# A two-layer hybrid decoder trunk on one NeuronCore: x^T kept by halves of K, one set of sum operands moved, two more weight load buffers

## The chip, the cores and the metric

The kernel runs on one core of one Trainium2 chip. TensorE (PE in the profile, its weight loads PEld), VectorE (DVE), ScalarE (ACT), GpSimd (POOL) and SyncE (SP) run their own instruction streams in order and meet through semaphores; 16 DMA engines move data between HBM and SBUF. SP issues one queue of DMAs and POOL another. The metric is device time in microseconds for the whole program. The kernel before takes 2170.99 us (median of 3 runs, 2167.93 to 2171.49). The profile is of one further execution, which took 2173.16 us.

## The reference

Two post-norm layers on 256 tokens of width 2048, all in float32:

```python
for i in range(DEPTH):                                  # DEPTH = 2
    mix = _hybrid_mixer(x, positions, w_in[i], g_cq[i], g_ckv[i], w_uq[i], w_ukv[i], w_o[i])
    x = _layer_norm(ALPHA * x + mix, ln1_g[i], ln1_b[i])
    ffn = _swiglu(x, w_gate[i], w_up[i], w_down[i])      # FFN_DIM = 5632
    x = _layer_norm(ALPHA * x + ffn, ln2_g[i], ln2_b[i])

def _swiglu(x, w_gate, w_up, w_down):
    h = silu(einsum('bsd,df->bsf', x, w_gate)) * einsum('bsd,df->bsf', x, w_up)
    return einsum('bsf,fd->bsd', h, w_down)
```

The mixer is one input projection, sparse attention over 64 selected keys, latent attention, and an output projection; the change does not touch its arithmetic. It bears on the feed-forward part (`_swiglu`).

## The kernel before

Precision comes from splitting: each float32 operand is a high part in float32r and a low part, and a product of two operands is three matmuls (high by high, high by low, low by high). ScalarE writes the high part of a weight tile (`wh`, line 336), VectorE subtracts it to get the low part (`wl`, line 337). A weight unit is 128 partitions x 1024 values, which is two K tiles of 128 by 512 columns, 512 KB.

**Buffers.** `load_raw` fetches a unit on SP's queue into a `raw` buffer. In the feed-forward part there are 8 of these: `RAW` = 4 that are there throughout and `RAWMORE` = 4 in a pool that is opened for this part (phase "more"). `some` deals them out by a fixed pattern. Seven `wh`/`wl` pairs (`UNITS` 5 and `MORE` 2) hold split units. `load_sum` fetches two units into a `sum` buffer on POOL's queue, the second added in flight; there are two such buffers. Eight-kilobyte tiles (`t8`) form a ring of 10: the two token tiles of x, x^T as `xh` and `xl` for both token tiles, one `few`, and the hidden activations `hT`.

**Feed-forward part.** FFN columns are cut into 11 chunks of 512 (`fc` 0 to 10). A chunk of gate and up is computed in four "quads", each taking one pair of K units, u and u + 4. A *plain* quad loads four units and uses each for both token tiles. A *sum* quad (`wino_quad`, "S") uses Winograd's form of Strassen: seven products instead of eight, each of one unit against one 128-token operand, p1, p2, p3, p6, p7, p4, p5 in this order. It loads three units (r11, r21, r22) and one sum (r12), and VectorE makes the other weights in place: r11 becomes r12 + r11 (line 1038), r21 becomes r11 + r21 (line 1045), r22 becomes r11 - r22 (line 1050). So the buffer of r11 is released only when line 1050 has read it. Some of the stationary operands are sums of quarters of x^T too; `sum_operands` makes them (`many` for K tiles 4 to 7, `few` for 2 and 3, a second `few` for 0 and 1). A *made* quad ("Q") reads weight sums that were made in the attention part and stored in HBM (`q`). Chunks 4 to 10 have the order S S Q S and use no plain quad; chunk 3 has S S plain S.

The products of a sum quad take as stationary operand token tile 0 with the low half of K (p1), token tile 0 with the high half (p2), token tile 1 with the high half (p4), and sums (the others). Token tile 1 with the low half of K is in no product of a sum quad.

From chunk 3 on, half of a `down` product (`down_half`, two columns of 512, 16 units, results added to x by POOL's DMAs `x<-d`) precedes each chunk's gate and up. `first_operands`, which makes the second `few`, is called between the two columns of the half before chunk 3.

**Order.** A list scheduler orders each engine's stream from the program's order, priorities and its own cost figures; `tc.high_priority` puts the closing VectorE additions of a chunk (`e`, `g`, line 1020) ahead. Streams are in order, so an instruction that waits holds back all behind it on its engine.

Of the kernel before, what the change touches and what calls it, by code (L numbers as in the profile page):

```python
# [25 lines left out]
F32R = mybir.dt.float32r  # L26
I32 = mybir.dt.int32
AF = mybir.ActivationFunctionType
ALU = mybir.AluOpType
# [3 lines left out]
P = 128  # L33
D = 2048
S = 256
NT = S // P
DEPTH = 2
# [15 lines left out]
KU = 2  # L53
C = 512
NKT = D // P
NFC = FFN // C
RAW = 4
UNITS, MORE = 5, 2
RAWMORE, RAWSUM = 4, 2
HALF = NKT // KU // 2  # L60
SOONER = 60
SOON = 200
# [2 lines left out]
ALLFROM, EARLY = 4, 0  # L65
# [17 lines left out]
def hybrid_trunk(ctx: ExitStack, tc: tile.TileContext, x, xt_in, pos, w_in, g_cq, g_ckv, w_uq,  # L83
                 w_ukv, w_o, ln1_g, ln1_b, ln1_T, w_gu, w_down, ln2_g, ln2_b, ln2_T, out):
    nc = tc.nc
# [7 lines left out]
    def nm(s):  # L93
        uid[0] += 1
        return f"{s}{uid[0]}"

    def t8(shape, dt, s):
        return sb.tile(shape, dt, name=nm(s), tag="a8", bufs=10)


    phase = {"name": None, "pool": None, "cm": None, "n": 0}
# [17 lines left out]
    def t2(shape, s, dt=F32):  # L119
        if phase["name"] == "att":  # L120
            phase["t2"] = phase.get("t2", 0) + 1
            if phase["t2"] * T2MORE % (T2 + T2MORE) < T2MORE:
                return pt(shape, dt, s, "t2", T2MORE)
        return sb.tile(shape, dt, name=nm(s), tag="t2", bufs=T2)
# [17 lines left out]
    def trp():  # L142
        return in_turn("tr", 4, 2)

    def att():

        return ps.tile([P, 2, C], F32, name=nm("att"), tag="b67", bufs=1)
# [3 lines left out]
    def f(ap):  # L151
        return ap.bitcast(F32)


    xt = [t8([P, D], F32, "x") for _ in range(NT)]
    xh = [t8([P, NKT, P], F32R, "xh") for _ in range(NT)]
    xl = [t8([P, NKT, P], F32R, "xl") for _ in range(NT)]

    def load_xT(u):

        ks = slice(KU * u, KU * u + KU)
        s = t2([P, NT, KU, P], "xs")
        nc.sync.dma_start(s, xt_in[u])
        for t in range(NT):
            split(xh[t][:, ks, :], xl[t][:, ks, :], s[:, t])

    def load_x():
        for t in range(NT):
# [100 lines left out]
    def step(task):  # L269
        try:  # L270
            task[0] = units_gone[0] + (next(task[1]) or 1)
        except StopIteration:
            tasks.remove(task)
# [7 lines left out]
    def spawn(gen):  # L281
        task = [0, gen]
        tasks.append(task)
        step(task)
        return task
# [90 lines left out]
    def transpose4(srcs, psum):  # L376
        for i, s in enumerate(srcs):
            nc.tensor.transpose(psum[:, i * P:(i + 1) * P], s, ident)  # L378

    def split(hi, lo, src):  # L380
        nc.scalar.activation(hi, src, AF.Copy)
        nc.vector.tensor_tensor(lo, src, f(hi), op=ALU.subtract)

    def xlhs(xh, xl):
        return lambda t, k: (xh[t][:, k, :], xl[t][:, k, :])

    def moments(y):

        st = small([P, D // C, 6], "bnst")
        for c in range(D // C):  # L390
            nc.vector.bn_stats(st[:, c, :], y[:, c * C:(c + 1) * C])
        mv = small([P, 2], "bnmv")
        nc.vector.bn_aggr(mv, st.rearrange("p c s -> p (c s)"))
        rs = small([P, 1], "bnrs")
        ve = small([P, 1], "bnve")
        nc.vector.tensor_scalar(ve, mv[:, 1:2], LN_EPS, None, ALU.add)
        nc.gpsimd.tensor_tensor(rs, ve, mhalf, op=ALU.pow)
        return mv[:, 0:1], rs

    def normalise(y, m):  # L400

        mu, rs = m
        for c in range(D // C):
            sl = slice(c * C, (c + 1) * C)
            nc.vector.tensor_scalar(y[:, sl], y[:, sl], mu, rs, ALU.subtract, ALU.mult)
            yield c, sl

    def norm_T(gbT, y, hi, lo, wait):


        for _ in normalise(y, moments(y)):
            pass
        yield wait
        pair = att()
        for c in range(D // C):
            tp = trp() if c < 2 else pair[:, c - 2, :]
            transpose4([y[:, c * C + i * P:c * C + (i + 1) * P] for i in range(4)], tp)
            v = t2([P, 4, P], "v")
            for i in range(4):
                k = 4 * c + i  # L420
                nc.scalar.activation(v[:, i, :], tp[:, i * P:(i + 1) * P], AF.Identity,
                                     bias=gbT[:, 1, k:k + 1], scale=gbT[:, 0, k:k + 1])
            nc.vector.tensor_copy(hi[:, 4 * c:4 * c + 4, :], v)
            nc.vector.tensor_tensor(lo[:, 4 * c:4 * c + 4, :], v, f(hi[:, 4 * c:4 * c + 4, :]), op=ALU.subtract)  # L424
            yield 1

    def load_gbT(src):
        gbT = sb.tile([P, 2, NKT], F32, name=nm("gbT"), tag="gbT", bufs=2)
        nc.gpsimd.dma_start(gbT, src)
        return gbT  # L430
# [97 lines left out]
        split(oh.rearrange("p j t -> p (j t)"), ol.rearrange("p j t -> p (j t)"), op)  # L528


    def layer(l, xh, xl, norms, last):
        xk = xlhs(xh, xl)

        def in_chunk(b, before=None, split_t=None):
            n = IN_BLOCKS[b][1]
# [303 lines left out]
        m = mla_half(0)  # L839
# [5 lines left out]
        m = mla_half(1)  # L845
# [20 lines left out]
        def many(shape):  # L866

            return phase["pool"].tile(shape, F32R, name=nm("many"), tag="many", bufs=1)
# [24 lines left out]
        finish(early)  # L893
        turn("more")
        gbT = load_gbT(ln1_T[l])
        xh, xl, norms = [], [], []

        def then(t):
            xh.append(t8([P, NKT, P], F32R, "xh"))
            xl.append(t8([P, NKT, P], F32R, "xl"))  # L900
            norms.append(spawn(norm_T(gbT, xt[t], xh[t], xl[t], 5 if t else 6)))

        last_pass(lambda c, k: w_o[l, c, k // KU], [4, 6], olhs, then)


        xk = xlhs(xh, xl)

        def gu(i, fc, split_t=None):
            return proj([(w_gu[i][l, fc, u], range(u * KU, (u + 1) * KU)) for u in range(NKT // KU)], xk, C,
# [1 line left out]

        sums = {}

        def sum_operands(*groups):


            for k0, n, where in groups:
                def x(t, i):
                    ks = slice(k0 + i * NKT // 2, k0 + i * NKT // 2 + n)
                    v = t2([P, n, P], "av")  # L920
                    nc.vector.tensor_tensor(v, f(xh[t][:, ks, :]), f(xl[t][:, ks, :]), op=ALU.add)
                    return v

                def diff(i, y, z):
                    v = t2([P, n, P], "sv")
                    nc.vector.tensor_tensor(v, y, z, op=ALU.subtract)
                    hi, lo = where[:, i, 0], where[:, i, 1]
                    split(hi, lo, v)
                    for k in range(n):
                        sums[f"s{i + 1}", k0 + k] = hi[:, k, :], lo[:, k, :]  # L930
                    return v

                a21 = x(1, 0)
                s1 = diff(0, a21, x(1, 1))
                a11 = x(0, 0)
                s2 = diff(1, a11, s1)
                diff(2, a21, a11)
                diff(3, x(0, 1), s2)
# [143 lines left out]
        def down(pair, cols, between=None):  # L1082


            fcs, hTs = [h[0] for h in pair], [h[1] for h in pair]
            finish(*[h[2] for h in pair])
            per = C // P // KU
            for i, c in enumerate(cols):
                o = proj([(w_down[l, c, per * fcs[0] + u], range(u * KU, (u + 1) * KU))
                          for u in range(per * len(fcs))], down_lhs(hTs), C, None, None, (0, 1) if i % 2 else (2, 3))  # L1090
                for t in range(NT):
                    d = t2([P, C], "d")
                    nc.scalar.activation(d, o[t], AF.Copy)  # L1093
                    nc.gpsimd.dma_start(xt[t][:, c * C:(c + 1) * C], d, accum_op=ALU.add)  # L1094
                if i == 0 and between:
                    between()
# [8 lines left out]
        held = []  # L1105
# [4 lines left out]
            held.append((fc, hT, spawn(hidden(g, u, hT, wait))))  # L1110

        def first_operands():
            sum_operands((0, 2, phase["pool"].tile([P, 4, 2, 2, P], F32R, name=nm("few"), tag="few", bufs=1)))

        def down_half(fc):

            down(held[:2], (0, 1) if fc % 2 else (2, 3), first_operands if fc == ALLFROM - 1 else None)
            if fc % 2 == 0:
                del held[:2]

# [6 lines left out]
        g = gu(0, 0, lambda: finish(*norms))  # L1127
        affine(ln1_g[l], ln1_b[l], 0, ALPHA)
        u = gu(1, 0)
        sum_operands((4, 4, many([P, 4, 2, 4, P])), (2, 2, t8([P, 4, 2, 2, P], F32R, "few")))  # L1130
        affine(ln1_g[l], ln1_b[l], 1, ALPHA)
        spawn_hidden(0, g, u)
        for fc in range(1, NFC):
            order = ORDER.get(fc, "SSQS")
            if fc >= FIRSTD:
                down_half(fc)
                finish_hidden()
            g, u = gate_up(fc, [({"N": "plain", "S": "wino", "Q": "made"}[k], v) for k, v in zip(order, UNIT[order])],
                           finish_hidden if fc < FIRSTD else None)
            if fc < FIRSTD:  # L1140
                affine(ln1_g[l], ln1_b[l], fc + 1, ALPHA)
            spawn_hidden(fc, g, u)
        xh, xl, norms, ms = [], [], [], []
        if last:
            gb = gains()
        else:
            gbT = load_gbT(ln2_T[l])
# [5 lines left out]
        if last:  # L1153
            for t in range(NT):
                norm_out(t, gb, ms[t])
        return xh, xl, norms

    norms = []
    for l in range(DEPTH):
        xh, xl, norms = layer(l, xh, xl, norms, l == DEPTH - 1)  # L1160
    turn(None)


# [48 lines left out]
```

## Time and profile before

| | |
|---|---|
| median of 3 runs | 2170.99 us |
| profiled execution | 2173.16 us |
| its span, first to last instruction | 2171.4 us |
| PE busy | 2139.9 us, 99% |
| DVE busy | 1848.9 us, 85% |
| ACT busy | 1288.8 us, 59% |
| POOL busy | 300.4 us, 14% |
| DMA queues, share of 16 engines | SP's 52.4%, POOL's 25.9% |
| mean granted TensorE clock | 0.997 |

A busy PE is not PE at its peak: matmuls overlap and their ends are modelled (a 512-column matmul is listed with 389 ns, but the next starts 227 ns later). So a stage's length says more than its busy share. Stages are cut here at the first matmul of a gate and up chunk (`gu_` tiles) and of a down half (`acc<-wh,hT`); chunks 4 to 10 of the first layer lie between 602 and 1012 us, those of the second between 1680 and 2092 us.

### The profile page before, as it was taken

The page shows a single profiled execution, that of the slowest core. Times are in us where ns is not written, and L with a number is a line of the kernel's source. Part 1 is how long each engine was busy: PE and PEld are TensorE (multiplying, and loading weights), DVE is VectorE, ACT ScalarE, POOL GpSimd, SP SyncE. Part 2 cuts the span into 40 slices and gives each one's busy share as a digit, 9 for nine tenths or more (in the row PEclk, how much of TensorE's full clock was granted, in tenths as well). Part 3 has the DMA queues.
Part 4 walks back from the last instruction along what each step waited for, and adds up shares of the span by engine and source line. Part 5 has one row for each costly group of instructions (what it writes and reads, how often), then busy time and mean ns, then how long its engine had stood idle before and what let it go on. Part 6 is the DMA issues. An engine that isn't in the chain of part 4 may idle for free.

```text
span 2171.4 us, 28387 instructions
## 1 busy us (share of the span) xinstructions
PE 2139.9 (99%) x9948; PEld 1768.8 (81%) x9948; DVE 1848.9 (85%) x2361; ACT 1288.8 (59%) x1675; POOL 300.4 (14%) x494
## 2 busy tenths in 40 slices
PE   8999999999999999999999999999999999999997
PEld 7888888888888878878888888888888888878876
DVE  6696776999989999999767976779998999989985
ACT  5555544666666667666455555446666666666663
POOL 0122220011011111110102122200011011111101
PEclk9999999999999999999999999999999999999999
DMA  8687888567888988887656877875678898888884
GB/s 299 206 295 273 294 292 280 175 203 244 260 258 265 281 266 267 269 281 255 203 180 227 292 275 280 315 247 174 210 250 256 272 270 261 275 266 268 286 311 106
DMA packets 158832, 552.97 MB, mean 255 GB/s; under 512 B 17904, under 2 KB 18208, under 8 KB 158048
## 3 DMA queue, kind: packets, MB, share of 16 engines
q1 hardware_dynamic: 111744, 401.79, 52.4%
q0 software_dynamic: 46800, 149.23, 25.9%
q8 instruction: 78, 1.28, 0.2%
q14 instruction: 66, 0.54, 0.1%
q10 hardware_dynamic: 144, 0.13, 0.0%
HBM read 498.12 MB, written 31.46 MB: 244 GB/s over the span
## 4 chain that ended last, share of the span: by engine, by line
PE 78%; DVE 11%; issue 5%; DMA 4%; ACT 1%; POOL 0%; SPq 0%; DVEq 0%; POOLq 0%; ACTq 0%
PE acc L359 16%; PE acc L358 16%; PE acc L360 16%; DVE wl L337 5%; PE gu_p L983 3%; PE gu_p L984 3%; PE gu_p L981 3%; DMA raw<-in_w_up_dram 3%; PE tr L378 2%; PE gu_c L981 2%; PE gu_c L984 2%; PE gu_c L983 2%; PE att L981 1%; PE att L984 1%; PE att L983 1%
## 5 line engine op out<-in xcount | busy, mean ns | idle before, releaser
L336 ACT ACTIVATE wh<-raw 128x1024 fp32r<-128x1024 f32 (+1 forms) x910 | 937.5, 1054 | 637.7 <-PE acc L360 220.9
L337 DVE TENSOR_TENSOR wl<-raw,wh 128x1024 fp32r<-128x1024 f32 (+1 forms) x910 | 1078.7, 1214 | 222.9 <-ACT wh L336 218.1
L358 PE MATMUL acc<-wh,xh 128*128 128x512 f32 (+1 forms) x768 | 302.9, 395 | 5.9 <-ACT wh L336 5.9
L359 PE MATMUL acc<-wl,xh 128*128 128x512 f32 (+1 forms) x768 | 297.5, 388 | 0.8 <-DVE wl L337 0.8
L360 PE MATMUL acc<-wh,xl 128*128 128x512 f32 (+1 forms) x768 | 297.4, 388 | 0.0
L359 PE MATMUL acc<-wl,hT 128*128 128x512 f32 x640 | 251.2, 392 | 0.5
L358 PE MATMUL acc<-wh,hT 128*128 128x512 f32 x640 | 250.0, 391 | 0.0
L360 PE MATMUL acc<-wh,hT 128*128 128x512 f32 x640 | 249.8, 390 | 0.0
L358 PEld LDWEIGHTS acc<-wh,xh 128*128 128x128 f32 x768 | 144.6, 188 | 37.0 <-ACT wh L336 7.1
L359 PEld LDWEIGHTS acc<-wl,xh 128*128 128x128 f32 x768 | 144.8, 189 | 28.9 <-DVE wl L337 2.9
L360 PEld LDWEIGHTS acc<-wh,xl 128*128 128x128 f32 x768 | 144.6, 188 | 28.3 <-DVE xl L424 0.6
L359 PEld LDWEIGHTS acc<-wl,hT 128*128 128x128 f32 x640 | 120.5, 188 | 30.4 <-DVE wl L337 5.8
L358 PEld LDWEIGHTS acc<-wh,hT 128*128 128x128 f32 x640 | 120.4, 188 | 25.3
L360 PEld LDWEIGHTS acc<-wh,hT 128*128 128x128 f32 x640 | 120.5, 188 | 24.7
L983 PE MATMUL gu_c<-wl,xh 128*128 128x512 f32 x360 | 140.3, 390 | 0.3 <-DVE wl L337 0.3
L981 PE MATMUL gu_c<-wh,xh 128*128 128x512 f32 x360 | 140.1, 389 | 0.0
L984 PE MATMUL gu_c<-wh,xl 128*128 128x512 f32 x360 | 140.1, 389 | 0.0
L1094 POOL DMA_DIRECT2D x<-d x80 | 69.5, 907 | 349.9 <-ACT d L1093 347.8
L315 POOL DMA_DIRECT2D sum<-in_w_up_dram x56 | 30.9, 552 | 533.6 <-DVE wl L337 501.6
L983 PE MATMUL gu_p<-wl,many 128*128 128x512 f32 x240 | 95.0, 396 | 8.6 <-DVE wl L337 8.4
L984 PE MATMUL gu_p<-wh,many 128*128 128x512 f32 x240 | 93.5, 390 | 0.0
L981 PE MATMUL gu_p<-wh,many 128*128 128x512 f32 x240 | 93.4, 389 | 0.0
(297 smaller groups left out, 3773.8 us busy)
## 6 DMA issues: line engine op xcount, KB each, us to landing
raw<-in_w_gate_dram SPq DMA_DIRECT2D x176, 512.0 KB, 5.9
raw<-in_w_down_dram SPq DMA_DIRECT2D x176, 512.0 KB, 7.7
raw<-in_w_in_dram SPq DMA_DIRECT2D x144, 512.0 KB, 5.2
sum<-in_w_up_dram POOLq DMA_DIRECT2D x112, 512.0 KB, 7.4
raw<-in_w_up_dram SPq DMA_DIRECT2D x106, 512.0 KB, 5.5
raw<-in_w_o_dram SPq DMA_DIRECT2D x64, 512.0 KB, 5.8
q<-q POOLq DMA_DIRECT2D x56, 512.0 KB, 4.1
raw<-q SPq DMA_DIRECT2D x56, 512.0 KB, 6.5
```

What stands on the lines that cost most here:

```text
L315: nc.gpsimd.dma_start(raw, a)
L336: nc.scalar.activation(wh[:, :n], raw[:, :n], AF.Copy)
L337: nc.vector.tensor_tensor(wl[:, :n], raw[:, :n], f(wh[:, :n]), op=ALU.subtract)
L358: mm(o[t][:, :n], h, a, start=first, stop=False)
L359: mm(o[t][:, :n], h, b, start=False, stop=False)
L360: mm(o[t][:, :n], l, a, start=False, stop=final)
L378: nc.tensor.transpose(psum[:, i * P:(i + 1) * P], s, ident)
L981: mm(o[name], h, a, start=name not in begun, stop=False)
L983: mm(o[name], h, b, start=False, stop=False)
L984: mm(o[name], l, a, start=False, stop=end)
L1094: nc.gpsimd.dma_start(xt[t][:, c * C:(c + 1) * C], d, accum_op=ALU.add)
```

## The change

x^T of a token tile is no longer one tile of high parts and one of low parts, each over all 16 K tiles, but one tile for the lower half of K and one for the upper, each with high and low parts (`halves`, `x_parts`). `first_operands` moves one chunk later, to the down half before chunk 4, and its tile (`few`, 8 KB) is no longer in the pool of the feed-forward part but a tile of the ring of 10, allocated after the first sum has read token tile 1 with the lower half of K. `RAWMORE` goes from 4 to 6: 10 raw buffers instead of 8, with the same 8 KB of the pool.

```diff
-RAWMORE, RAWSUM = 4, 2
+RAWMORE, RAWSUM = 6, 2
...
-    xh = [t8([P, NKT, P], F32R, "xh") for _ in range(NT)]
-    xl = [t8([P, NKT, P], F32R, "xl") for _ in range(NT)]
+
+    def halves():
+
+        return [t8([P, 2, NKT // 2, P], F32R, "xhl") for _ in range(2)]
+
+    xT = [halves() for _ in range(NT)]
+
+    def x_parts(x, k, n):
+
+        ks = slice(k % (NKT // 2), k % (NKT // 2) + n)
+        return tuple(x[k // (NKT // 2)][:, i, ks, :] for i in range(2))
...
-    def xlhs(xh, xl):
-        return lambda t, k: (xh[t][:, k, :], xl[t][:, k, :])
+    def xlhs(xT):
+        return lambda t, k: tuple(m[:, 0, :] for m in x_parts(xT[t], k, 1))
...
+        def few():
+            return t8([P, 4, 2, 2, P], F32R, "few")
+
         def sum_operands(*groups):
 
 
-            for k0, n, where in groups:
+            for k0, n, place in groups:
                 def x(t, i):
-                    ks = slice(k0 + i * NKT // 2, k0 + i * NKT // 2 + n)
                     v = t2([P, n, P], "av")
-                    nc.vector.tensor_tensor(v, f(xh[t][:, ks, :]), f(xl[t][:, ks, :]), op=ALU.add)
+                    hi, lo = x_parts(xT[t], k0 + i * NKT // 2, n)
+                    nc.vector.tensor_tensor(v, f(hi), f(lo), op=ALU.add)
                     return v
...
                 a21 = x(1, 0)
+                where = place()
                 s1 = diff(0, a21, x(1, 1))
...
         def first_operands():
-            sum_operands((0, 2, phase["pool"].tile([P, 4, 2, 2, P], F32R, name=nm("few"), tag="few", bufs=1)))
+
+            sum_operands((0, 2, few))
 
         def down_half(fc):
 
-            down(held[:2], (0, 1) if fc % 2 else (2, 3), first_operands if fc == ALLFROM - 1 else None)
+            down(held[:2], (0, 1) if fc % 2 else (2, 3), first_operands if fc == ALLFROM else None)
...
-        sum_operands((4, 4, many([P, 4, 2, 4, P])), (2, 2, t8([P, 4, 2, 2, P], F32R, "few")))
+        sum_operands((4, 4, lambda: many([P, 4, 2, 4, P])), (2, 2, few))
```

PE's instructions keep their order throughout. On VectorE, the place to look at is the first layer's sum quad that is split ahead while a down half runs. Before, in the half before chunk 3 (`raw_5130`, `raw_5132`, `raw_5134` are that quad's r11, r21, r22; `av` and `sv` are the sums of x^T, `few` their low parts):

```order
L1038 TENSOR_TENSOR raw_5130<-sum_5127,raw_5130 128x1024
L921 TENSOR_TENSOR av_5009<-xh_3781,xl_3782 128x256
L921 TENSOR_TENSOR av_5011<-xh_3781,xl_3782 128x256
L337 TENSOR_TENSOR wl_5159<-raw_5134,wh_5158 128x1024
L926 TENSOR_TENSOR sv_5013<-av_5009,av_5011 128x256
L1045 TENSOR_TENSOR raw_5132<-raw_5130,raw_5132 128x1024
L382 TENSOR_TENSOR few_5008<-sv_5013,few_5008 128x256
```

Now, in the half before chunk 4 (`raw_5642`, `raw_5644`, `raw_5646` are r11, r21, r22 of chunk 4's first quad):

```order
L1049 TENSOR_TENSOR raw_5642<-sum_5639,raw_5642 128x1024
L931 TENSOR_TENSOR av_5520<-xhl_3781 128x256
L931 TENSOR_TENSOR av_5523<-xhl_3782 128x256
L345 TENSOR_TENSOR wl_5671<-raw_5646,wh_5670 128x1024
L936 TENSOR_TENSOR sv_5525<-av_5520,av_5523 128x256
L1056 TENSOR_TENSOR raw_5644<-raw_5642,raw_5644 128x1024
L390 TENSOR_TENSOR few_5522<-sv_5525,few_5522 128x256
```

The twelve operations on x^T moved as a block by one chunk; the weight operations between them stand as they did.

On SP, the end of chunk 4's loads in the first layer. Before (`raw_5810` to `raw_5814` and the `q` loads are the made quad, `raw_5897`, `raw_5899`, `raw_5901` the last sum quad's r11, r21, r22):

```order
L309 DMA raw_5850<-q_1317 128x1024
L309 DMA raw_5852<-q_1315 128x1024
L309 DMA raw_5899<-in_w_gate_dram 128x1024
L309 DMA raw_5897<-in_w_gate_dram 128x1024
L309 DMA raw_5901<-in_w_up_dram 128x1024
L309 DMA raw_5991<-in_w_down_dram 128x1024
L309 DMA raw_6009<-in_w_down_dram 128x1024
```

Now:

```order
L317 DMA raw_5850<-q_1317 128x1024
L317 DMA raw_5852<-q_1315 128x1024
L317 DMA raw_5897<-in_w_gate_dram 128x1024
L317 DMA raw_5899<-in_w_gate_dram 128x1024
L317 DMA raw_5991<-in_w_down_dram 128x1024
L317 DMA raw_5901<-in_w_up_dram 128x1024
L317 DMA raw_6009<-in_w_down_dram 128x1024
```

r11 stands first again, and the quad's third load has one `down` load moved ahead of it. Elsewhere on this queue single neighbours trade places in the same way.

On VectorE, the end of the first layer's attention part, where the last units of `w_o` are split (`own` tiles hold two of them). Before:

```order
L337 TENSOR_TENSOR own_3594<-raw_3601,own_3594 128x1024
L337 TENSOR_TENSOR wl_3420<-raw_3417,wh_3419 128x1024
L337 TENSOR_TENSOR own_3605<-raw_3612,own_3605 128x1024
L337 TENSOR_TENSOR wl_3438<-raw_3435,wh_3437 128x1024
L337 TENSOR_TENSOR wl_3460<-raw_3457,wh_3459 128x1024
```

Now, some ten rows later in VectorE's stream:

```order
L345 TENSOR_TENSOR wl_3577<-raw_3574,wh_3576 128x1024
L345 TENSOR_TENSOR own_3594<-raw_3601,own_3594 128x1024
L345 TENSOR_TENSOR wl_3587<-raw_3584,wh_3586 128x1024
L345 TENSOR_TENSOR own_3605<-raw_3612,own_3605 128x1024
L345 TENSOR_TENSOR wl_3598<-raw_3595,wh_3597 128x1024
```

The two `own` splits stand about ten rows later than before.

## Rows read from the trace of the kernel before

**Rows 1.** Page, part 1: busy us (share of the span) xinstructions.

```profile
PE 2139.9 (99%) x9948; PEld 1768.8 (81%) x9948; DVE 1848.9 (85%) x2361; ACT 1288.8 (59%) x1675; POOL 300.4 (14%) x494
```

**Rows 2.** Windows, gate/up chunks 4-10: length, busy by engine, PEclk, DMA share, GB/s.

```profile
910.92:951.32 40.40, 38.61 (x172) 31.46 (x170) 37.21 (x35) 28.69 (x32) 4.78 (x7) 1.00 0.85 267
974.26:1012.43 38.17, 38.17 (x171) 31.62 (x169) 37.44 (x36) 30.44 (x33) 1.69 (x2) 1.00 0.75 242
...
sum 547.79, PE 538.96 PEld 441.37 DVE 505.31 ACT 395.43 POOL 60.59; mean PE 38.50 PEld 31.53 DVE 36.09 ACT 28.25 POOL 4.33
```

**Rows 3.** Windows, the down halves before chunks 4 to 10, both layers.

```profile
579.63:602.19 22.56, 22.56 (x105) 18.76 (x104) 19.04 (x17) 11.29 (x14) 3.08 (x4) 1.00 0.78 242
...
702.43:725.14 22.71, 22.71 (x106) 18.68 (x104) 22.41 (x22) 13.97 (x18) 2.87 (x5) 1.00 0.95 289
...
sum 319.69, PE 319.24 PEld 261.70 DVE 304.05 ACT 180.18 POOL 42.16; mean PE 22.80 PEld 18.69 DVE 21.72 ACT 12.87 POOL 3.01
```

**Rows 4.** Windows, the closing down product of the first and of the second layer.

```profile
1012.43:1058.24 45.81, 45.81 (x207) 37.99 (x206) 32.70 (x30) 25.98 (x31) 5.59 (x7) 1.00 0.95 302
2091.97:2139.53 47.56, 47.56 (x207) 38.95 (x206) 30.96 (x29) 25.49 (x31) 6.19 (x8) 0.96 0.72 215
```

**Rows 5.** Timeline of PE at chunk 9's end: start, us, operation [idle before <-releaser].

```profile
950.06 0.50 PE L983 MATMUL gu_p<-wl,many 128*128 128x512 f32 x1 [1.79 <-DVE wl L337]
```

**Rows 6.** Timeline of DVE, last sum quad of chunk 9.

```profile
935.75 1.23 DVE L337 TENSOR_TENSOR wl<-raw,wh 128x1024 fp32r<-128x1024 f32 x1 [1.05 <-ACT wh L336]
938.34 1.23 DVE L337 TENSOR_TENSOR wl<-raw,wh 128x1024 fp32r<-128x1024 f32 x1 [1.36 <-ACT wh L336]
939.48 1.22 DVE L1038 TENSOR_TENSOR raw<-sum,raw 128x1024 f32<-128x1024 f32 x1
...
948.79 1.21 DVE L337 TENSOR_TENSOR wl<-raw,wh 128x1024 fp32r<-128x1024 f32 x1
```

**Rows 7.** Timeline of ACT, the same quad.

```profile
930.29 1.07 ACT L336 ACTIVATE wh<-raw 128x1024 fp32r<-128x1024 f32 x1 [0.23 <-PE gu_p L984]
931.65 1.06 ACT L336 ACTIVATE wh<-raw 128x1024 fp32r<-128x1024 f32 x1 [0.29 <-PE gu_p L984]
934.66 1.06 ACT L336 ACTIVATE wh<-raw 128x1024 fp32r<-128x1024 f32 x1 [1.95 <-DMA raw<-in_w_gate_dram]
937.25 1.06 ACT L336 ACTIVATE wh<-raw 128x1024 fp32r<-128x1024 f32 x1 [1.52 <-PE gu_p L984]
```

**Rows 8.** Timeline of SP's queue, chunk 9: start of the first, us to the last, loads.

```profile
910.65 14.10 SPq L309 DMA_DIRECT2D raw<-q  x4
925.65 1.47 SPq L309 DMA_DIRECT2D raw<-in_w_gate_dram  x2
927.92 0.33 SPq L309 DMA_DIRECT2D raw<-in_w_up_dram  x1
```

**Rows 9.** Waits of SP's queue, whole span: us in total, times, longest.

```profile
SPq L309 <- DVE raw L1050: 525.0, 54, 18.8
```

**Rows 10.** Windows inside chunk 9.

```profile
914.00:923.00 9.00, 9.00 (x41) 7.48 (x40) 9.00 (x9) 5.20 (x5) 1.41 (x2) 1.00 0.92 221
...
941.00:947.00 6.00, 6.00 (x28) 4.83 (x27) 6.00 (x6) 5.27 (x6) 0.56 (x1) 1.00 0.37 129
```

**Rows 11.** Windows, the down half before chunk 3.

```profile
517.49:540.06 22.57, 22.57 (x106) 18.77 (x104) 21.83 (x28) 11.91 (x16) 2.27 (x3) 1.00 0.67 221
```

**Rows 12.** Waits of DVE, 517 to 541 us.

```profile
DVE sv L926 <- DMA x<-d: 0.6, 1, 0.6
```

**Rows 13.** Tile d, 500 to 610 us and 605 to 1000 us: the DMAs `x<-d`.

```profile
DMA to landing us min/median/max: 3.5/5.0/9.6
...
DMA to landing us min/median/max: 6.1/8.3/11.5
```

**Rows 14.** Tile own, 320 to 390 us: PE's first use; timeline of DVE before it.

```profile
L885 PE MATMUL acc<-own,oA x8: 389/389/395, 371.4 to 386.6; 128*128 128x512 f32 x8
...
359.62 2.44 DVE L337 TENSOR_TENSOR wl<-raw,wh 128x1024 fp32r<-128x1024 f32 x2 [1.32 <-ACT wh L336]
```

More of the change, by code (lines that the diff above doesn't have):

```diff
@@ L155, in hybrid_trunk @@
     xt = [t8([P, D], F32, "x") for _ in range(NT)]
-    xh = [t8([P, NKT, P], F32R, "xh") for _ in range(NT)]
-    xl = [t8([P, NKT, P], F32R, "xl") for _ in range(NT)]
+    def halves():
[4 more added lines that the diff above has]
+        return tuple(x[k // (NKT // 2)][:, i, ks, :] for i in range(2))
     def load_xT(u):
-        ks = slice(KU * u, KU * u + KU)
         s = t2([P, NT, KU, P], "xs")
@@ L164, in load_xT @@
         for t in range(NT):
-            split(xh[t][:, ks, :], xl[t][:, ks, :], s[:, t])
+            split(*x_parts(xT[t], KU * u, KU), s[:, t])
     def load_x():
@@ L406, in normalise, with norm_T @@
             yield c, sl
-    def norm_T(gbT, y, hi, lo, wait):
+    def norm_T(gbT, y, xT, wait):
         for _ in normalise(y, moments(y)):
@@ L422, in norm_T @@
                                      bias=gbT[:, 1, k:k + 1], scale=gbT[:, 0, k:k + 1])
-            nc.vector.tensor_copy(hi[:, 4 * c:4 * c + 4, :], v)
-            nc.vector.tensor_tensor(lo[:, 4 * c:4 * c + 4, :], v, f(hi[:, 4 * c:4 * c + 4, :]), op=ALU.subtract)
+            hi, lo = x_parts(xT, 4 * c, 4)
+            nc.vector.tensor_copy(hi, v)
+            nc.vector.tensor_tensor(lo, v, f(hi), op=ALU.subtract)
             yield 1
@@ L528, in attend, with layer @@
         split(oh.rearrange("p j t -> p (j t)"), ol.rearrange("p j t -> p (j t)"), op)
-    def layer(l, xh, xl, norms, last):
-        xk = xlhs(xh, xl)
+    def layer(l, xT, norms, last):
+        xk = xlhs(xT)
         def in_chunk(b, before=None, split_t=None):
@@ L895, in layer @@
         gbT = load_gbT(ln1_T[l])
-        xh, xl, norms = [], [], []
+        xT, norms = [], []
         def then(t):
-            xh.append(t8([P, NKT, P], F32R, "xh"))
-            xl.append(t8([P, NKT, P], F32R, "xl"))
-            norms.append(spawn(norm_T(gbT, xt[t], xh[t], xl[t], 5 if t else 6)))
+            xT.append(halves())
+            norms.append(spawn(norm_T(gbT, xt[t], xT[t], 5 if t else 6)))
         last_pass(lambda c, k: w_o[l, c, k // KU], [4, 6], olhs, then)
-        xk = xlhs(xh, xl)
+        xk = xlhs(xT)
         def gu(i, fc, split_t=None):
@@ L1142, in layer @@
             spawn_hidden(fc, g, u)
-        xh, xl, norms, ms = [], [], [], []
+        xT, norms, ms = [], [], []
         if last:
@@ L1155, in layer @@
                 norm_out(t, gb, ms[t])
-        return xh, xl, norms
+        return xT, norms
     norms = []
     for l in range(DEPTH):
-        xh, xl, norms = layer(l, xh, xl, norms, l == DEPTH - 1)
+        xT, norms = layer(l, xT, norms, l == DEPTH - 1)
     turn(None)
```

## The prediction

> **What bounds the kernel now.** I read part 1 of the page first. PE is busy 2139.9 of 2171.4 us [rows 1], so nothing that shortens another engine's work can help unless PE waits for it, and all that can be won lies in the places where PE stands still. To find them I cut the feed-forward part into stages, because a stage's length shows a stall that the busy share hides. The 14 gate and up chunks with the order S S Q S (chunks 4 to 10, both layers) have the same matmuls, and their lengths differ: the shortest takes 38.17 us, the longest 40.40 [rows 2]. The shortest shows what PE needs when it waits for nobody.
>
> What ends the wait is read on PE at the end of the longest chunk, chunk 9 of the first layer: the second matmul of its last product starts at 950.06 after waiting 1.79 us for a `wl` split [rows 5]. So DVE is late there, and the question is why, since DVE has slack over a whole period. Following DVE back from that split (948.79 [rows 6]) it works without a gap to 938.34, and before that it was idle twice, 1.05 and 1.36 us, for ACT's high parts. ACT in turn [rows 7]: the splits at 930.29 and 931.65 are 1.36 apart, which is PE's pace of one product (six matmuls of 0.227), because seven `wh`/`wl` pairs circulate and each waits for PE to leave one. At that pace the next two would have come at 933.0 and 934.4. They came at 934.66, waiting for a load by name, and at 937.25. The trace puts the second wait down to PE, but its pair was free at about 934.4 by the count of seven; its load was issued only at 927.92 [rows 8], so I take it to be the load again, 2.85 us late.
>
> Why were these loads late? SP's queue [rows 8]: the four `q` loads of the made quad took from 910.65 on 14.1 us to issue, and the last quad's three loads came behind them at 925.65, 926.79 (the second of a pair that takes 1.47 with its 0.33 issue) and 927.92. SP is held by `raw L1050`, 525 us over the span in 54 waits, up to 18.8 [rows 9]: with eight buffers in turn, the third `q` load needs the buffer of the second sum quad's r11, eight loads back, which DVE gives back with line 1050, late in that quad. Then ten loads leave in a burst and the last quad's stand third to fifth in it. So in these chunks the number of raw buffers bounds the loads, the loads DVE, and DVE the last product.
>
> **The change part by part.** *Two more raw buffers.* With ten, the third and fourth `q` load take buffers two loads older, of the first sum quad, and the last quad's r11 waits for line 1050 instead. Its three loads issue two places earlier, some 2.3 us (925.65 against about 923.3), and have two loads fewer in front of them. In chunk 9, 2.85 us is what the late loads cost ACT; PE's stall is 40.40 - 38.17 = 2.23. If the loads are in time, all of DVE's unbroken work from 938.34 on moves 2.85 earlier, and the split that PE waited for (done 950.0, wanted at 948.1) is done by 947.2. The stall goes whole, with 0.9 to spare. What is late next is DVE's own work: in the shortest chunk it is busy 37.44 of 38.17 without a stall for PE [rows 2], so it suffices, barely.
>
> The sum over all places, each against the shortest stage of its kind:
> - gate and up: 547.79 - 14 x 38.17 = 13.4 us [rows 2];
> - down halves: of the 14, the two before chunk 4 (22.56) follow no S S Q S chunk. The other twelve take 319.69 - 2 x 22.56 = 274.6, against 12 x 22.71 (the one behind a chunk with no stall) = 272.5, which leaves 2.1 [rows 3]; it is the first split of the half, behind the same late DVE work;
> - clock: the closing down product takes 47.56 in the second layer and 45.81 in the first, at a granted clock of 0.96 and 1.00 [rows 4]. PE stood still just before it in the second layer (that chunk is one of the long ones), so I count these 1.75 us with the stalls.
>
> Together 17.2 us, from 17 places. From this I take off 1.4 (0.1 per chunk, since DVE stays close to PE) and the two items below.
>
> *The moved sums.* Twelve small DVE operations leave the half before chunk 3 and go to the half before chunk 4, in each layer. The first half has DVE busy 21.83 in 28 instructions, the second 19.04 in 17 [rows 3, 11]; the sums are twelve of the former, so with one split less (1.2) they are about 4.0 us. The half before chunk 4 has 22.56 - 19.04 = 3.5 us in which DVE is idle, so the sums lie beside PE's work but for 0.5. One of them (`sv`) takes a buffer of the `x<-d` transfers of the first column; before, it waited 0.6 us for one [rows 12], when these land after 5.0 us (median) [rows 13]. Bounds: below, the sums cost nothing, since chunk 3 gives back what chunk 4 takes (a gain of 0, for the half before chunk 3 has no stall, 22.57 against 22.56); above, the transfers land after 11.5 us [rows 13] and DVE stands 6.5 longer, in each layer. I take the row as it is, 0.5 + 0.6 in each layer, and since the new buffers leave some slack in chunk 4, half of it: 1.1 for both.
>
> *x^T by halves.* As many instructions, of the same shapes, and PE's order is the same; the operands of DVE's additions lie in one tile instead of two. I take 0. At the program's start a copy of 256 columns now goes ahead of ACT's first weight split of 1024 columns (1.07 [rows 7]): between 0 and 1.07, by columns 0.3, and I leave it within the rounding.
>
> *Order at the layer's middle.* The two `own` splits stand ten rows later. PE first wants one at 371.4, and the row that now stands ahead of the first begins at 359.62 [rows 14], so nine microseconds cover it; if their loads came late by more than that, PE would wait. I take 0.
>
> 17.2 - 1.4 - 1.1 = 14.7 less: 2173.16 becomes 2158.5 for an execution with a profile. The runs before have their median 2.2 below that execution, so the median should be 2170.99 - 14.7, about **2156.3**.
>
> **A rule of the Trainium skill that speaks against it.** Inside chunk 9 the DMA engines have a share of 0.92 from 914 to 923, while SP is held and moves almost nothing, and 0.37 from 941 to 947 [rows 10]. The first is POOL's traffic, sums and `x<-d`. The Trainium skill, "DMA: Bandwidth & Descriptors", section "Issuing engines are not separate DMA queues", says that DMAs of all issuing engines run on the same 16 engines and interleave, so that a further issuer gains no bandwidth. By that rule alone the two `q` loads that go earlier take their time from POOL's transfers, and this is the first rival.
>
> **The rivals.**
> 1. *The 16 engines are full.* For it: the share of 0.92 at just the time where the loads go, and 0.95 in a down half [rows 3, 10]. Against it: 0.37 six microseconds long in the same chunk, 0.75 over the shortest chunk [rows 2], and the loads that go early are not new bytes. If POOL's transfers and the two loads share what was there, the last quad's loads gain the two places and not the engines' time: about half of the 17.2, less the sums: a median near 2164.
> 2. *The loads are in time, and DVE is late anyway.* For it: DVE is busy 37.21 in the longest and 37.44 in the shortest chunk. If the seven pairs, not the loads, had held ACT at 937.25, as the trace's name says, only the 1.65 of 934.66 would be gained by ACT and lost again at 937.25. Then nothing comes of it but a microsecond or two: 2170. The same time follows if the scheduler hands out ten buffers so that the held load stays behind line 1050.
> 3. *Slower: `x<-d` holds the moved sums.* Place: the half before chunk 4. The extra loads and `x<-d` compete, the transfers land as late as 11.5 instead of 5.0, and `sv` holds DVE in order, and behind it the splits of chunk 4's first quad. Each microsecond beyond a landing of 5 costs PE up to one, in each layer: 6.5 + 1.1 twice is 15, and half that as a middling case, 7.5, gives 2178. It decides only where the buffers bring less than that, so with rival 2.
>
> **How the numbers follow.** Forecast 0.58 (2152 to 2161), rival 1 0.22 (2160 to 2167), rival 2 0.13 (2167 to 2172), rival 3 0.07. About 0.2%, 4.3 us, is what a measurement of this kernel can tell from no change: so faster 0.80, no change 0.14, slower 0.06. The range runs from the whole 17.2 with 1.5 for the runs' spread, 2152.5, to 2168, which takes in rival 1 and the edge of rival 2 and leaves out the rest, less than 0.2.
>
> **What would show it.** Right: `raw L1050` falls in SP's waits by well over half in chunks 4 to 10; ACT's waits for loads there go; the 14 chunks take 38.2 to 38.5 each; no fall of the clock before the closing product of the second layer. Rival 1: loads issue earlier but take longer to land, and ACT still waits for them. Rival 2: ACT's wait at that place stays, by PE's name, with its load long landed. Rival 3: chunk 4 of the first layer longer than it is now, with a DVE wait for `x<-d` ahead of it. I am wrong outright if chunks 5 to 10 keep their lengths.

## The result and the profile after

The changed kernel takes **2153.48 us** (median of 6 runs, 2152.57 to 2154.43), the kernel before 2170.1 in the same comparison: ratio 0.9924, interval [0.9912, 0.9937], 16.6 us less. The profiled execution took 2152.57 us.

Page of the changed kernel, part 1; PE's 2139.9 [rows 1] has become 2129.1, the other engines' work is what it was:

```profile
PE 2129.1 (99%) x9948; PEld 1769.6 (82%) x9948; DVE 1847.1 (86%) x2361; ACT 1293.2 (60%) x1675; POOL 302.4 (14%) x494
```

Windows of the changed kernel, columns as in [rows 2]: chunk 9 of the first layer, chunk 10 of the second and the sum of the fourteen; the halves before chunk 3 and before chunk 4 and the sum of the fourteen halves before chunks 4 to 10; the two closing down products; a stretch of the second layer's attention:

```profile
906.15:944.33 38.18, 38.18 (x172) 31.63 (x170) 37.40 (x36) 29.11 (x33) 4.48 (x6) 1.00 0.90 282
2034.92:2073.10 38.18, 38.18 (x172) 31.63 (x170) 37.40 (x36) 29.12 (x33) 3.14 (x5) 1.00 0.94 317
sum 534.71, PE 534.71 PEld 442.75 DVE 521.97 ACT 414.76 POOL 60.31; mean PE 38.19 PEld 31.62 DVE 37.28 ACT 29.63 POOL 4.31
...
517.59:540.15 22.56, 22.56 (x105) 18.76 (x104) 19.03 (x17) 11.29 (x14) 3.11 (x4) 1.00 0.74 245
579.69:602.33 22.64, 22.64 (x106) 18.78 (x104) 21.81 (x28) 11.90 (x16) 2.24 (x3) 1.00 0.70 218
sum 315.97, PE 315.97 PEld 262.62 DVE 294.44 ACT 167.52 POOL 42.02; mean PE 22.57 PEld 18.76 DVE 21.03 ACT 11.97 POOL 3.00
...
1005.12:1050.89 45.77, 45.77 (x207) 37.99 (x206) 32.72 (x30) 26.94 (x32) 6.18 (x8) 1.00 0.93 301
2073.10:2118.95 45.85, 45.85 (x208) 37.93 (x207) 30.49 (x29) 24.89 (x30) 6.20 (x8) 1.00 0.67 198
...
1216.07:1229.28 13.21, 11.80 (x61) 8.95 (x59) 13.11 (x37) 5.96 (x14) 4.67 (x9) 1.00 1.00 362
```

The last of these stretches in the kernel before:

```profile
1223.43:1238.84 15.41, 13.42 (x60) 9.93 (x59) 14.83 (x38) 6.00 (x14) 3.88 (x10) 0.89 0.99 363
```

In the chunks and halves PE's busy time now equals the length: it stands still nowhere. The ledger of the two profiled executions: chunks 547.79 - 534.71 = 13.1; halves 319.69 - 315.97 = 3.7; closing products 93.37 - 91.62 = 1.75; attention 2.2; together 20.75 against 20.6 between the spans. The last 2.2 us the change doesn't touch: in that one execution of the kernel before the granted clock was 0.89 in the stretch. The profiled execution of the kernel before lies 3.1 above the median of its kernel and the one after 0.9 below; these 4.0 stand between the 20.6 of the profiles and the 16.6 of the medians, so part of the ledger belongs to that one execution and not to the kernel.

ACT at the place of [rows 7], chunk 9 of the first layer, in the changed kernel (timeline):

```profile
926.85 1.06 ACT L344 ACTIVATE wh<-raw 128x1024 fp32r<-128x1024 f32 x1 [0.30 <-PE gu_p L995]
928.21 1.06 ACT L344 ACTIVATE wh<-raw 128x1024 fp32r<-128x1024 f32 x1 [0.30 <-PE gu_c L995]
929.57 1.06 ACT L344 ACTIVATE wh<-raw 128x1024 fp32r<-128x1024 f32 x1 [0.30 <-PE att L995]
```

The three splits stand 1.36 apart, at PE's pace; the waits for loads, 1.95 and 1.52 long in [rows 7], are gone. SP's queue of the changed kernel for the same quad (timeline), and its waits over the whole span:

```profile
918.48 1.43 SPq L317 DMA_DIRECT2D raw<-in_w_gate_dram  x2
920.88 0.33 SPq L317 DMA_DIRECT2D raw<-in_w_up_dram  x1
```

```profile
SPq L317 <- DVE raw L1061: 495.7, 54, 18.5
```

Counted from the chunk's start (906.15, before 910.92) the quad's three loads issue at 12.3, 13.4 and 14.7, before [rows 8] at 14.7, 15.9 and 17.0: two places earlier, as forecast. But SP waits for line 1061 (1050 before) almost as long as ever, 495.7 against 525.0 over the span [rows 9], 341.5 against 370.2 in chunks 4 to 10. The wait has not gone; another load stands in it: the first of the last quad's loads now goes out at 12.3, where the third `q` load did. I had written this myself ("the last quad's r11 waits for line 1050 instead"), so the sign I named, a fall by well over half, contradicted my own working. It is the one sign that didn't come, and it is where the experiments start: what is it that the two places bring?

### The profile page after: what moved, and what is told of

It is laid out like the page before. It is cut to its first block, busy times and chain, and to the rows that moved or that the text cites. A ratio compares the mean times of both kernels' runs of the same rounds, so it can differ in the third digit from the quotient of the medians.

```text
span 2150.8 us, 28402 instructions
## 1 busy us (share of the span) xinstructions
PE 2129.1 (99%) x9948; PEld 1769.6 (82%) x9948; DVE 1847.1 (86%) x2361; ACT 1293.2 (60%) x1675; POOL 302.4 (14%) x494
## 4 chain that ended last, share of the span: by engine, by line
PE 91%; DVE 6%; issue 2%; POOL 1%; DMA 0%; ACT 0%; POOLq 0%; DVEq 0%; SPq 0%; ACTq 0%
PE acc L366 16%; PE acc L367 16%; PE acc L368 16%; PE gu_p L992 6%; PE gu_p L995 6%; PE gu_p L994 6%; PE gu_c L995 4%; PE gu_c L992 4%; PE gu_c L994 4%; PE att L995 2%; PE att L992 2%; PE att L994 2%; PE tr L386 2%; DVE wl L345 2%; PE acc L894 1%
## 5 line engine op out<-in xcount | busy, mean ns | idle before, releaser
L366 PE MATMUL acc<-wh,xhl 128*128 128x512 f32 (+1 forms) x768 | 303.0, 395 | 6.8 <-ACT wh L344 6.8
L368 PE MATMUL acc<-wh,xhl 128*128 128x512 f32 (+1 forms) x768 | 297.7, 388 | 0.0
L367 PE MATMUL acc<-wl,xhl 128*128 128x512 f32 (+1 forms) x768 | 297.6, 388 | 0.0
L366 PEld LDWEIGHTS acc<-wh,xhl 128*128 128x128 f32 x768 | 144.7, 189 | 37.3 <-ACT wh L344 7.6
L368 PEld LDWEIGHTS acc<-wh,xhl 128*128 128x128 f32 x768 | 144.8, 188 | 28.5 <-DVE xhl L432 0.6
L367 PEld LDWEIGHTS acc<-wl,xhl 128*128 128x128 f32 x768 | 144.9, 189 | 28.0 <-DVE wl L345 1.9
L992 PE MATMUL gu_c<-wh,xhl 128*128 128x512 f32 x360 | 140.1, 389 | 0.0
L995 PE MATMUL gu_c<-wh,xhl 128*128 128x512 f32 x360 | 140.1, 389 | 0.0
L994 PE MATMUL gu_c<-wl,xhl 128*128 128x512 f32 x360 | 140.0, 389 | 0.0
```

The source lines that it names most:

```text
L366: mm(o[t][:, :n], h, a, start=first, stop=False)
L367: mm(o[t][:, :n], h, b, start=False, stop=False)
L368: mm(o[t][:, :n], l, a, start=False, stop=final)
L992: mm(o[name], h, a, start=name not in begun, stop=False)
L994: mm(o[name], h, b, start=False, stop=False)
L995: mm(o[name], l, a, start=False, stop=end)
```

## The experiments

**8 buffers again, the rest of the change kept.**

```diff
-RAWMORE, RAWSUM = 6, 2
+RAWMORE, RAWSUM = 4, 2
```

> The changed kernel with 8 raw buffers instead of 10: x^T by halves and the moved sums alone. Theory (loads issued late for want of raw buffers): all stalls at the chunk ends are back, the 14 chunks 4 to 10 take together 545 to 550 us, 2168 to 2174 us in all. Rival (layout and moved sums bring part of the gain themselves): under 2165. Rival 3 (x<-d holds the moved sums): over 2174, chunk 4 of the first layer over 40 us.

Measured 2168.41 us, ratio to before 0.9999 [0.999, 1.0007]. The stalls are back (the fourteen chunks take 545.0 in its profile, 534.7 with ten buffers): the layout with the moved sums is worth nothing by itself, and the gain hangs on the buffers.

**x^T by halves alone.**

```diff
-RAWMORE, RAWSUM = 6, 2
+RAWMORE, RAWSUM = 4, 2
...
-            sum_operands((0, 2, few))
+            pool = phase["pool"]
+            sum_operands((0, 2, lambda: pool.tile([P, 4, 2, 2, P], F32R, ...)))
...
-first_operands if fc == ALLFROM else None
+first_operands if fc == ALLFROM - 1 else None
```

> x^T by halves alone: 8 raw buffers, the sums of x^T back in the half before chunk 3 and in the pool. Every engine's order as before, as far as names tell. Theory: 2168 to 2172 us, the layout costs and brings nothing. Rival (the layout in one tile makes VectorE's additions faster or slower): under 2165 or over 2174.

Measured 2174.23 us, ratio 1.0026 [1.0015, 1.0036]: 4.6 slower, where the rival's number was, but not by its reason: VectorE's additions of x^T take 420 ns (median) in both kernels. What stands out in the profile is one chunk, the last of the second layer. A second profile of this kernel was to tell whether that is its own:

> A second profile of x^T by halves alone. If the 43.19 us of chunk 10 in the second layer is that kernel's own, it stands here again within 1 us and accounts for most of its 4.6 us; if it is an accident of one execution, that chunk takes under 41 and the 4.6 us lies spread over the stalls.

Windows of that chunk in the two profiles of this kernel, one fence each (before: 40.28):

```profile
2049.80:2093.00 43.20, 39.56 (x171) 31.36 (x170) 37.45 (x35) 28.79 (x32) 3.71 (x6) 1.00 0.84 290
```

```profile
2049.50:2092.42 42.92, 39.53 (x171) 31.52 (x170) 37.61 (x35) 28.94 (x32) 3.71 (x6) 1.00 0.84 294
```

It is this kernel's own. POOL's timeline has the cause: the last layer's gains (`gall`, `ball`, 1 MB each, in tiles of the ring of 10). With x^T by halves alone (first fence) the second `ball` goes out with the first, at 2059.47; with the moved sums (the run moved8, second fence) 19 us later, and in the kernel before (third fence) 21.5 us behind the first (2061.77).

```profile
2059.47 1.42 POOL L460 DMA_DIRECT2D ball<-in_ln_b_dram  x2
```

```profile
2059.57 0.55 POOL L460 DMA_DIRECT2D ball<-in_ln_b_dram  x1 [4.21 <-PE gu_p L995]
2078.61 0.54 POOL L460 DMA_DIRECT2D ball<-in_ln_b_dram  x1 [18.49 <-PE gu_p L995]
```

```profile
2083.30 0.54 POOL L452 DMA_DIRECT2D ball<-in_ln_b_dram  x1 [20.98 <-PE gu_c L984]
```

The last quad's three loads then take 11.7 to 12.0 us to land, 8.8 to 9.1 before and 6.8 to 7.1 in moved8. By the program, the layout frees a tile of the ring sooner. Left free, it lets a megabyte start 4.6 us ahead of these loads; when `few` takes it, it doesn't, and that chunk takes 38.28 us in moved8. So a transfer lengthens this chunk, not VectorE's work. That it is all of the 4.6 us isn't shown: against the profile before, the chunk is 2.9 longer. Against the run narrow8 below, where it takes 38.20 and the closing product behind it 45.83, chunk and product are 6.7 longer (43.19 and 47.56) and the execution 6.6.

**9 buffers.**

```diff
-RAWMORE, RAWSUM = 6, 2
+RAWMORE, RAWSUM = 5, 2
```

> The changed kernel with 9 raw buffers. Theory: the last quad's r11 takes the buffer of r21 of the second sum quad instead of r22 (8) or r11 (10), so its loads stand between: about half of the gain, 2158 to 2164 us. If the pairs of split units or the 16 DMA engines set the pace (rivals 2 and 1), the ninth buffer does as little as nothing: 2166 to 2171.

Measured 2155.98 us, ratio 0.9939 [0.9925, 0.9953]: 13.6 of 16.6 us, more than the half I expected. Of the fourteen chunks two are left with a stall to speak of, chunk 7 in each layer; in the first it takes 39.05 (window):

```profile
784.22:823.27 39.05, 38.53 (x172) 31.55 (x170) 35.38 (x33) 28.18 (x31) 4.47 (x6) 1.00 0.83 259
```

Its last load is issued at 799.92, 0.22 behind an accumulating sum load of POOL's (799.70), and takes long. DMA issues between 799.6 and 800.0 (KB each, us to landing), this kernel:

```profile
sum<-in_w_up_dram POOLq DMA_DIRECT2D x1, 512.0 KB, 10.1
raw<-in_w_gate_dram SPq DMA_DIRECT2D x1, 512.0 KB, 9.7
```

The load before it, issued 0.9 ahead of the sum load, landed after 5.8. (In four other chunks of this kernel the third load goes out within 0.4 of the sum load, too, takes 8.6 to 8.8 and lands 24.5 to 24.7 us after the chunk's start, and these chunks take 38.2 to 38.3; in this one it lands at 25.4.) That pointed at a theory of its own, tested below.

**Eight pairs instead of ten buffers.**

```diff
-UNITS, MORE = 5, 2
-RAWMORE, RAWSUM = 6, 2
+UNITS, MORE = 5, 3
+RAWMORE, RAWSUM = 4, 2
```

> The changed kernel with 8 raw buffers and eight wh/wl pairs instead of seven: the 8 KB go to a pair. Theory: the last quad's loads are as late as before, ScalarE still waits for them, less than a third of the gain: 2164 to 2171 us. Rival 2 (the seven pairs hold ScalarE): all or most of the gain, 2153 to 2158.

Measured 2179.82 us, ratio 1.0052 [1.0039, 1.0064]: 10 slower than before, which neither theory said. The fourteen chunks take 547.4, as before (547.8): a pair more does not bring the splits in time, which speaks against rival 2. By itself it doesn't settle it, since the edit changes VectorE's and ScalarE's order as well. The loss stands in the halves, 326.9 against 319.7; part of it is a new wait of PE's first product in a chunk for ScalarE's `d` copy, up to 1.6 us.

**The other side: six pairs with ten buffers.**

```diff
-UNITS, MORE = 5, 2
+UNITS, MORE = 5, 1
```

> The changed kernel with its 10 raw buffers and six wh/wl pairs instead of seven. Theory (loads alone were the limit): under 2162 us, chunks 5 to 10 at 38.2 to 38.6. Rival (once loads are in time the pairs are the next limit): 2170 or more, ScalarE waiting for TensorE's release of a pair and TensorE for a split.

Measured 2159.17 us, ratio 0.9951 [0.9938, 0.9964]: three fifths of the gain with a pair fewer. Chunks 5 to 10 take 38.2, so with loads in time even six pairs hold nothing there: with pair8, this is what puts rival 2 out. Most of what is lost stands in the halves, 319.9 against 316.0, the larger part of it in those before chunk 4 (24.1 and 23.9).

**VectorE reads r11 for the last time sooner, 8 buffers, kernel before.**

```diff
                 if not made:
                     nc.vector.tensor_tensor(r21, r11, r21, op=ADD)
+                    nc.vector.tensor_tensor(r22, r11, r22, op=SUB)
                 p("p7", slhs("s3"), r7, lo_)
...
-                if not made:
-                    nc.vector.tensor_tensor(r22, r11, r22, op=SUB)
                 p("p4", token(1), r4, hi_)
```

> The kernel before with 8 raw buffers, no change but one: VectorE's line that reads r11 for the last time (r22 = r11 - r22) is written directly behind r21 = r11 + r21, one or two VectorE operations (1.2 to 2.4 us) sooner. SP's, POOL's and TensorE's order stay. Theory: the held q load and the last quad's three loads issue that much earlier, half of the stalls or more go, 2156 to 2164 us. Rivals 1 and 2 (full DMA engines, pairs): 2167 to 2172, since neither bytes nor pairs change. Slower than 2172 if the operation taken forward holds the split that TensorE wants.

Measured **2151.89 us**, ratio 0.9919 [0.9905, 0.9934]: the whole gain, without a buffer more. But not for the reason I gave. Only the third `q` load issues sooner (11.2 instead of 12.3 after the chunk's start); the last quad's three issue at 14.6, 15.7 and 16.8, where they were at 14.7, 15.9 and 17.0. They only land sooner. In VectorE's stream the line changed places with the split of the sum buffer (timeline at chunk 9's second quad, before and then this kernel):

```profile
920.84 1.22 DVE L337 TENSOR_TENSOR wl<-sum,wh 128x1024 fp32r<-128x1024 f32 x1
921.98 1.21 DVE L1050 TENSOR_TENSOR raw<-raw,raw 128x1024 f32<-128x1024 f32 x1
```

```profile
914.73 1.22 DVE L1046 TENSOR_TENSOR raw<-raw,raw 128x1024 f32<-128x1024 f32 x1
915.87 1.22 DVE L337 TENSOR_TENSOR wl<-sum,wh 128x1024 fp32r<-128x1024 f32 x1
```

That split releases a sum buffer, so POOL's next sum load starts one operation later. POOL's timeline, before and then this kernel:

```profile
922.35 0.56 POOL L315 DMA_DIRECT2D sum<-in_w_up_dram  x1 [2.85 <-DVE wl L337]
927.39 0.84 POOL L316 DMA_DIRECT2D sum<-in_w_up_dram  x1 [4.48 <-DMA sum<-in_w_up_dram]
```

```profile
917.39 0.56 POOL L315 DMA_DIRECT2D sum<-in_w_up_dram  x1 [10.28 <-DVE wl L337]
923.19 0.84 POOL L316 DMA_DIRECT2D sum<-in_w_up_dram  x1 [5.24 <-DMA sum<-in_w_up_dram]
```

From the chunk's start (910.92, here 904.82) the accumulating half goes out at 16.5 before, between the quad's second and third load, and at 18.4 here, behind all three.

**The rival of the full DMA engines, in its first form: thin `x<-d`, kernel before.**

```diff
-nc.gpsimd.dma_start(xt[t][:, c * C:(c + 1) * C], d, accum_op=ALU.add)
+n = C // 8
+nc.gpsimd.dma_start(xt[t][:, c * C:c * C + n], d[:, :n], accum_op=ALU.add)
```

> The kernel before, where each x<-d DMA adds 64 of its 512 columns (an eighth of the bytes; the rest of the down product's additions is left out). Rival 1 (the 16 DMA engines are full): the loads land in time, 2152 to 2160 us. Theory (SP is held by a buffer): the last quad's loads issue as late as before, most stalls stay, 2163 to 2171 us; the part that goes is the time a load takes in the burst.

Measured 2167.61 us, ratio 0.9991 [0.9982, 1.0]: no difference. The bytes of `x<-d` are not what the loads meet: in the kernel before, chunk 9's two go out at 910.3 and 911.2 and land 9.9 to 11.0 later, by 922.3, and the first of the last quad's loads goes out at 925.65. Of POOL's traffic, which rival 1 names, this leaves the sum loads.

**Its second form: the accumulating half of the sum load, kernel before.**

```diff
-nc.gpsimd.dma_start(raw, b, accum_op=ALU.add)
+n = KU * C // 8
+nc.gpsimd.dma_start(raw[:, :n], b[:, :n], accum_op=ALU.add)
```

> The kernel before with 8 raw buffers, where the second, accumulating DMA of each sum load adds 128 of its 1024 columns (the rest of the sum of weights is left out). All instructions keep their order. New theory (the last quad's second and third load land behind the accumulating sum load, which is issued 15.5 to 16 us after the chunk's start, in the middle of them): they land at 21 to 23 us after the chunk's start instead of 23.6 to 26, the stalls of chunks 4 to 9 go, and the time is 2151 to 2158 us; what stays is chunk 10 of the second layer, which has no such load. The theory of the prediction (late issue for want of a buffer is the whole of it): issue times stay, so the stalls stay, 2164 to 2171.

Measured **2153.63 us**, ratio 0.9931 [0.9919, 0.9944]. This decides it, together with early8: here every sum load is thinned and none is shifted, there all bytes stay and one sum load starts later (and one `q` load earlier). SP's queue stands as before (timeline; chunk 9 starts at 905.80, so 14.7, 15.8 and 17.0), SP's wait for r11's buffer nearly so, and the stall is gone, here (window) and in chunks 4 to 9 of both layers, each 38.2:

```profile
920.48 1.47 SPq L309 DMA_DIRECT2D raw<-in_w_gate_dram  x2
922.75 0.33 SPq L309 DMA_DIRECT2D raw<-in_w_up_dram  x1
```

```profile
SPq L309 <- DVE raw L1051: 498.2, 54, 18.7
```

```profile
905.80:943.98 38.18, 38.18 (x171) 31.59 (x169) 37.45 (x36) 29.10 (x32) 4.48 (x6) 1.00 0.76 258
```

What changed is how long the same loads take. DMA issues around the last quad of chunk 9, second load, sum load, third load: the kernel before, this one, and the changed kernel, in which the sum load goes out last:

```profile
raw<-in_w_gate_dram SPq DMA_DIRECT2D x1, 512.0 KB, 7.8
sum<-in_w_up_dram POOLq DMA_DIRECT2D x1, 512.0 KB, 9.1
raw<-in_w_up_dram SPq DMA_DIRECT2D x1, 512.0 KB, 8.9
```

```profile
raw<-in_w_gate_dram SPq DMA_DIRECT2D x1, 512.0 KB, 6.2
sum<-in_w_up_dram POOLq DMA_DIRECT2D x1, 64.0 KB, 6.9
...
raw<-in_w_up_dram SPq DMA_DIRECT2D x1, 512.0 KB, 6.4
```

```profile
raw<-in_w_gate_dram SPq DMA_DIRECT2D x1, 512.0 KB, 5.0
...
raw<-in_w_up_dram SPq DMA_DIRECT2D x1, 512.0 KB, 5.0
...
sum<-in_w_up_dram POOLq DMA_DIRECT2D x1, 512.0 KB, 9.3
```

In chunk 10 of the first layer, which had no stall before (38.17 [rows 2]), no sum load follows, since no chunk is left to load for, and the second and third load land after 5.6 and 5.8. But a late landing isn't always a stall. Chunk 5 of the first layer took 38.20 before, though its sum load goes out at 15.8 and its second and third load land 23.6 and 25.5 us after its start, against 23.6 and 25.9 in chunk 9 (40.40). In the five profiles with 8 buffers, seven pairs and neither cure, chunk 5 takes 38.2 to 38.4 and chunk 9 39.8 to 40.4; what in a chunk sets how much of the lateness reaches PE stays open. Chunk 10 of the second layer, where I expected the stall to stay, took 38.70 us here; in moved8 it took 38.28, before 40.28. There the loads meet the gains, by an amount that differs from profile to profile.

**Both cures, 10 buffers and the early line.** The edit of early8 on the changed kernel.

> The changed kernel, 10 raw buffers, with the early r22 = r11 - r22 of the run early8 added. Both theories: no stall at a chunk's end is left to win, 2150 to 2154 us, the same as either alone. Rival (VectorE is tight: the operation taken forward holds a split that TensorE wants): over 2156.

Measured 2153.54 us, ratio 0.9928 [0.9915, 0.9942]. Every chunk takes 38.2: nothing is left to win at the chunks' ends. early8 has the lowest median of all, but the 1.6 us between it and the changed kernel are under what a measurement of this kernel tells.

## Why the prediction was right, and where it was not

The time, 2153.48, lies 2.8 below the 2156.3 forecast, and inside the range. The sum was read from the lengths of PE's stages, so it holds for any means that brings the loads in by time; I had only half of the reason why two buffers are such a means, and to that extent the hit is luck.

- *Where the time was to be had* was right, place by place: the stall at a chunk's end goes whole (13.1 measured, 13.4 forecast), the fall of the clock after it too (1.75). The halves gave 3.7 instead of 2.1: I had measured them against a half of 22.71, and the undisturbed ones take 22.56. Of these terms, the stall in chunk 10 of the second layer (2.1) and the fall of the clock behind it may belong to the one execution I read: in narrow8 and moved8, with 8 buffers too, that chunk takes 38.2 and 38.3.
- *The deductions* were not needed. VectorE close to PE was to cost 1.4; the chunks take 38.19 on average, 0.02 over the shortest. The moved sums were to cost 1.1; the half before chunk 4 takes 22.64 against 22.56 for the others, and `sv` waits for `x<-d` as before (0.6 [rows 12]):

```profile
DVE sv L936 <- DMA x<-d: 0.7, 1, 0.7
```

- *Why the loads were late* is the step that failed. I wrote that "the number of raw buffers bounds the loads", with SP held as the reason, and gave the DMA engines' load to a rival that would halve the gain. The held queue is half of it: it decides when the last quad's loads go out. That the second and third then land some 2 to 3 us late is the accumulating half of a sum load, issued 15.5 to 16.5 us into the chunk. Thin it (sumnarrow8) or let it start later (early8), and 8 buffers are enough, with SP held nearly as long as before in the one case (498.2) and issue times within 0.2 us of before in both. Two buffers more do it by the other end: the first two loads go out ahead of the sum load, at 12.3 to 13.1 and 13.4 to 14.2, in most chunks the third too (14.6 to 14.7). In five of the twelve chunks 4 to 9 the third still goes out at 15.7 to 16.4 and takes 6.5 to 8.8, without a stall. So rival 1 had the right resource, shared with POOL's traffic, but did not tell the sum loads, which the last loads meet, from `x<-d`, which they don't (narrow8). Its sum was wrong: it gave half of the gain, and moving the loads ahead of the sum load gave all of it.
- *The rule* I had weighed there, the Trainium skill's "DMA: Bandwidth & Descriptors", section "Issuing engines are not separate DMA queues" (DMAs of all issuing engines share 16 engines and interleave), agrees with these runs: the same load of SP's took 8.9 us beside POOL's 512 KB and 6.4 beside 64 KB. What I drew from it was not.
- *x^T by halves at nothing* was wrong taken alone: 4.6 us slower with 8 buffers, 2.9 of it, against the profile before, by a transfer that the freed tile lets start. In the change `few` holds that tile, so no term of the sum shows it. I had priced instructions and not who gets the freed space.
- *Rival 2* fell with pair8 and pair6raw10, *rival 3* with the `sv` wait above and with moved8, where chunk 4 of the first layer takes 39.23 (before 39.22). The clock: in the profiles where the second layer's last chunk took over 40 us (before 40.28, layout8 43.2 and 42.9), the closing product behind it took 47.3 to 47.6; where it took 38.2 to 38.7 (moved8, narrow8, pair8, sumnarrow8), 45.8 to 46.2. So the 1.75 went with that stall. Why an equal stall in chunk 9 of the first layer (40.40, clock 1.00 [rows 2]) brought no fall stays open.

## What to carry to other kernels

When an engine waits for a load, read two times of it apart: when it was issued and how long it took to land. A queue held by a buffer explains only the first; if the same issue times give other landings, look at what the other queue issued within a microsecond of it. A cure by space (two buffers) and a cure by order (one line of VectorE moved, which shifts when another engine's transfer starts) can then be worth the same, and the second needs no space. A late landing costs only what exceeds the slack behind it, so read the stall at the engine that waits, too. And price what a freed tile lets start, not only what it holds.

## What I had not expected

A 512 KB load issued 0.9 us ahead of a 512 KB accumulating load landed after 5.8 us, one issued 0.2 behind such a load after 9.7. One DMA issued within a microsecond of two loads, in chunks 4 to 9 of both layers, goes with 11.3 us of stall (against chunks of 38.17) in the profiled execution of a kernel whose PE was busy 99% of the span.
